# The chunk inverse of a bidirectional recurrence: 64x64 corners of the array, with the transpose carried along

## The chip, the cores and the metric

One core of a Trainium2 chip runs the whole program. The metric is the device time in microseconds (us) of one execution. TensorE is called PE here (its weight loads PEld), VectorE DVE, ScalarE ACT, GpSimd POOL and SyncE SP, as the profile names them.

## The reference, cut to what matters

The reference is an encoder trunk of two layers on 256 tokens of 1024 channels, in float32: a bidirectional RWKV-7 recurrence, a mixture of experts, a dilated attention, a second mixture of experts. Only the recurrence is touched. For each of 16 heads of 64 channels and for both directions it computes

```python
def step(state, inp):
    r_t, w_t, k_t, v_t, a_t, b_t = inp
    sa = jnp.einsum('bhvk,bhk->bhv', state, a_t)
    state = (state * w_t[:, :, None, :]
             + sa[:, :, :, None] * b_t[:, :, None, :]
             + v_t[:, :, :, None] * k_t[:, :, None, :])
    y_t = jnp.einsum('bhvk,bhk->bhv', state, r_t)
    return state, y_t
```

## The kernel before

The 256 tokens of a head and direction are cut into four chunks of 64. Inside a chunk the steps depend on each other through a strictly triangular 64x64 matrix A, so the kernel works out (1 - A)^-1 of each chunk, and the recurrence (`recur`, L963) then goes over only four chunks. Heads go in pairs, i = 0 to 7: two heads, two directions and four chunks are 16 inverses of 64x64 in one call of `inverse` (L882). They lie as 8 numbers n by two halves q of the 128 partitions, 64 columns each.

`chunks` (L828) leaves A in two half-precision parts. Before the change these tiles, Ah and Al (L690), are 128 wide: half q has its 64x64 block at columns 64q, so that tile [:, n, :] is a 128x128 matrix with two blocks on the diagonal, and zero elsewhere (cleared once by POOL, L692). Ah has had 1 subtracted (L853). `inverse` keeps T, the transposed inverse of ever larger blocks, 64 columns wide (`plain`, L895, an ACT copy from PSUM to half precision), and TTd, the same matrix not transposed and spread onto the diagonal (`spread`, L904, two ACT copies of one half each). Each of the levels l = 1 to 5 does: T from PSUM; for l > 1 a turn of T on PE (`turn`, L890: 16 matmuls of 64x64 weights against an identity) and its spread into TTd; Ah times T (`pairs`, L885: 8 matmuls with 128x128 weights and 64 columns); Q, that product under the level's mask, by DVE (L929); TTd times Q. At the end T is turned once more into X, the residual is taken with Ah and Al, split into TTd and Td, and two terms of its series are added (L954 to L960).

Work of several kinds is woven in the recurrence's phase (`weave`, L272, loop at L1158). Turn i has the streams steps(i) = recur(i) and then ready(i + 2) (scaled operands and chunk products), inverse(i + 1), finish(i - 1) (head norm, gate), and supply(i + 3) (the projections kr and v of a later pair, and shares of the modulations). Each emits its pieces with a priority that follows its share of PE's work (SHARE, L33), and a scheduler sets each engine's order at build time from those priorities. All engines run in that order. Names in the rows: iv is a PSUM bank of the inverse, cst (or cst16) the constants, kr and v the projections, wring the ring of weights, G the chunk products, R, U, S, Y the recurrence's banks, bb and sT the bonus, Al and Ah the parts of A, wo the output projection, gu and dn the experts' products. All matmuls are issued by one helper, at L266. A float32 matmul stands in the profile as two records.

The ring of weights (`Stream`, L120) gets more memory as tiles of this phase are given back (`later`, L1810, at i = 4, 5, 6, 7 and the end). The experts' weights, 1 MB a block, go into it.

Of the kernel before, what the change touches and what calls it, by code (L numbers as in the profile page):

```python
# [12 lines left out]
F16 = mybir.dt.float16  # L13
# [18 lines left out]
# share of the tensor engine's work of the streams that are woven, and their offset in priority  # L32
# [13 lines left out]
def _constants():  # L46
# [3 lines left out]
    parts = {}  # L50
# [4 lines left out]
    # from here on for the recurrence only  # L55
# [52 lines left out]
def _attn_constants():  # L108
    """Negative distances under the masks of the three groups; the tokens in the order even, odd."""
# [10 lines left out]
class Stream:  # L120
    """Blocks of weights, in the order in which they are used, through a ring of tiles.

    While a phase leaves room, a second pool lengthens the ring for the blocks before `limit`."""
# [38 lines left out]
    def spare(self):  # L162
        """A tile of the ring, once it holds all the blocks that are left."""
# [8 lines left out]
    def take(self, *names):  # L172
        """The next blocks; those taken before are used up."""
# [8 lines left out]
    def done(self):  # L182
        """The blocks taken last are used up."""
# [7 lines left out]
# modulations (layer, kind, eighth) that are worked out before and during each token mixer  # L191
# [45 lines left out]
def trunk(ctx, tc, names, aps, out, stages=("rwkv", "moe0", "attn", "moe1"), dbg=None, ring=2):  # L237
# [16 lines left out]
    def banks(**n):  # L254
        """The banks of PSUM of a phase, by their uses."""
# [16 lines left out]
    def weave(*streams):  # L272
        """Emits streams side by side, each in step with its share of the tensor engine's work."""
# [87 lines left out]
    def ada_first(tag, acc):  # L361
        """Shift and scale of the first norm, by both engines."""
# [23 lines left out]
    def ada(i, m, k, tag="ps"):  # L386
        """An eighth of one of the six modulations."""
# [31 lines left out]
    def split(hi, lo, src, by, eng=None):  # L419
        """src times `by` (a power of two) as the sum of two numbers in half precision"""  # L420
# [12 lines left out]
    def scales(i, which):  # L433
        """columns of the modulated norm: scale, shift"""
# [23 lines left out]
    def normalised(xn, tags):  # L458
        """the normalised stream in [d, t], two eighths of the channels in a bank each"""
# [17 lines left out]
    def transposed(j, behind=False):  # L477
        """a quarter of the stream's channels in [d, t]"""
# [9 lines left out]
    class Router:  # L488
        """Logits of the router, as the parts of x come in: its scale per token is put to the products."""
# [5 lines left out]
        def start(self):  # L495
            """The scaled weights, the part of the shift."""
# [14 lines left out]
        def hold(self, tag):  # L511
            """The bank and the sums that the parts of x go to."""
# [3 lines left out]
        def feed(self, t, c, junk):  # L516
            """a tile of tokens, half of the channels"""
# [23 lines left out]
    def gated(w, gate, k):  # L541
        """the rows of an output projection (k blocks side by side), times the gates of its columns"""
# [8 lines left out]
    def add_out(ps, t, c, by=1.0):  # L551
        """x += ps * by, in half of the channels of a tile of tokens"""
# [5 lines left out]
    def ada_share(n, tag="ps"):  # L558
        """The next n eighths of the modulations that go with layer 0."""
# [5 lines left out]
    def rwkv(pool):  # L565
# [4 lines left out]
        # (what the even pairs of heads use is given back before what the odd ones use)  # L570
# [5 lines left out]
        def pieces(tag):  # L576
            """tiles that are used before the recurrence needs their places"""
# [36 lines left out]
        # (past the ends lies a zero, which the shift does not move)  # L614
# [36 lines left out]
        def hidden():  # L651
            """LoRA hidden layers, [rank, t]"""
# [33 lines left out]
        E16, N16, R16 = cst16[:, 0:128], cst16[:, 128:256], cst16[:, 256:320]  # L686
        lv = cst16[:, 320:704].rearrange("p (l n) -> p l n", l=6)
        lv0 = cst16[:, 704:832]
        # (two matrices of 64 x 64 each, on the diagonal)
        Td, TTd, *A16 = [inv.tile([128, 8, 128], F16, name=n)  # L690
# [1261 lines left out]
```

## Time and profile before

| what | value |
|---|---|
| runs of the kernel | 1224.38, 1223.29 and 1211.89 us, median 1223.29 |
| span of the profiled execution | 1225.3 us (no time of that execution is given beside it) |
| PE, matmuls | 1086.9 us busy, 89%, 9460 records |
| PE, weight loads | 725.7 us, 59% |
| DVE | 660.5 us, 54% |
| ACT | 449.9 us, 37% |
| POOL | 177.8 us, 15% |
| mean granted PE clock | 0.936 |

Matmuls are pipelined and their ends modelled, so the distance between starts says what a matmul costs, not its own duration. The recurrence's phase is about the first 500 us; the experts of layer 0 follow to about 720 us, the attention to about 1000 us, the experts of layer 1 to the end.

### The profile page before, as it was taken

The page shows a single profiled execution, that of the slowest core. Times are in us where ns is not written, and L with a number is a line of the kernel's source. Part 1 is how long each engine was busy: PE and PEld are TensorE (multiplying, and loading weights), DVE is VectorE, ACT ScalarE, POOL GpSimd, SP SyncE. Part 2 cuts the span into 40 slices and gives each one's busy share as a digit, 9 for nine tenths or more (in the row PEclk, how much of TensorE's full clock was granted, in tenths as well). Part 3 has the DMA queues.
Part 4 walks back from the last instruction along what each step waited for, and adds up shares of the span by engine and source line. Part 5 has one row for each costly group of instructions (what it writes and reads, how often), then busy time and mean ns, then how long its engine had stood idle before and what let it go on. Part 6 is the DMA issues. An engine that isn't in the chain of part 4 may idle for free. (4 is left out here: it accounts for less than half of the span.)

```text
span 1225.3 us, 22879 instructions
## 1 busy us (share of the span) xinstructions
PE 1086.9 (89%) x9460; PEld 725.7 (59%) x9460; DVE 660.5 (54%) x1453; ACT 449.9 (37%) x940; POOL 177.8 (15%) x128
## 2 busy tenths in 40 slices
PE   4679999999999899897988879899988998799886
PEld 4556777777777664543443258778877864354432
DVE  8875477787774733522121166989986563122112
ACT  3326454464562552210010066546544531011002
POOL 6600001001120610000000012212283200000000
PEclk8789999999995999898998989989998999999989
DMA  9253164344352055898999996887653498989995
GB/s 373 101 206 117 35 204 125 123 156 133 106 173 103 2 241 221 333 422 352 422 421 421 420 419 240 315 319 290 237 197 138 168 361 358 417 366 421 421 420 229
DMA packets 53188, 322.46 MB, mean 263 GB/s; under 512 B 5922, under 2 KB 6562, under 8 KB 21458
## 3 DMA queue, kind: packets, MB, share of 16 engines
q1 hardware_dynamic: 51986, 316.49, 66.3%
q0 software_dynamic: 512, 2.30, 0.5%
q10 hardware_dynamic: 576, 2.10, 0.5%
q8 instruction: 78, 1.28, 0.4%
q14 instruction: 36, 0.29, 0.1%
HBM read 319.82 MB, written 1.05 MB: 262 GB/s over the span
## 5 line engine op out<-in xcount | busy, mean ns | idle before, releaser
L266 PE MATMUL gu<-wring,xT 128*32 128x512 f32 x1024 | 132.5, 619 | 16.9 <-DMA wring<-in_w_moe_dram 9.9
L358 DVE SCALAR_TENSOR_TENSOR acc<-aring,silu,acc 128x512 f32<-128x512 f32 x140 | 114.4, 849 | 9.5 <-DMA aring<-in_w_ada_dram 9.3
L425 POOL TENSOR_TENSOR wl<-wring,wh 128x1024 f16<-128x1024 f32 x24 | 57.2, 2383 | 407.1 <-DMA wring<-in_w_qkv_dram 241.0
L266 PE MATMUL qkv<-hl,wh 128*128 128x256 f16 x384 | 106.3, 277 | 2.0 <-DVE hl L1614 2.0
L266 PE MATMUL qkv<-hh,wl 128*128 128x256 f16 x384 | 106.4, 278 | 1.8 <-DVE wl L431 1.8
L266 PE MATMUL qkv<-hh,wh 128*128 128x256 f16 x384 | 106.6, 278 | 1.6 <-ACT hh L1613 1.6
L266 PEld LDWEIGHTS gu<-wring,xT 128*32 128x32 f32 x1024 | 31.8, 112 | 99.9 <-issue 80.4
L266 PEld LDWEIGHTS <-wh 128*128 128x128 f16 x768 | 76.4, 100 | 13.1 <-issue 3.6
L431 DVE SCALAR_TENSOR_TENSOR wl<-wring,wh 128x1024 f16<-128x1024 f32 x56 | 74.0, 1327 | 16.4 <-ACT wh L427 16.3
L266 PE MATMUL dn<-wring,hidT 128*32 128x256 f32 x1024 | 66.3, 407 | 18.1 <-ACT hidT L1416 18.0
L266 PE MATMUL acc<-y,back 128*128 128x512 f32 (+1 forms) x144 | 66.0, 581 | 10.3 <-DVE y L1443 8.1
L427 ACT ACTIVATE wh<-wring 128x1024 f16<-128x1024 f32 x56 | 58.6, 1050 | 35.4 <-PE qkv L266 30.8
L266 PEld LDWEIGHTS xT<-oh,x 128*128 128x128 f32 x512 | 59.0, 192 | 21.1 <-issue 9.2
L1218 DVE SCALAR_TENSOR_TENSOR sg<-sg,gu 128x256 f32<-128x256 f32 x16 | 6.7, 420 | 119.1 <-ACT sg L1217 119.1
L1443 DVE TENSOR_TENSOR y<-dn,ga 128x512 f32<-128x512 f32 x28 | 19.4, 692 | 88.9 <-PE dn L266 57.4
L266 PE MATMUL xT<-oh,x 128*128 128x128 f32 x512 | 63.5, 280 | 2.5 <-DVE oh L1327 2.5
L1217 ACT ACTIVATE sg<-gu 128x256 f32<-128x256 f32 x16 | 6.1, 383 | 153.1 <-PE gu L266 153.1
L266 PEld LDWEIGHTS dn<-wring,hidT 128*32 128x32 f32 x1024 | 32.1, 116 | 48.5 <-ACT hidT L1416 21.9
L1359 ACT ACTIVATE back<-bT 128x256 f32<-128x256 f32 x16 | 6.1, 384 | 131.7 <-PE acc L266 131.7
L266 PE MATMUL qkv<-wl,hh 128*128 128x256 f16 x192 | 54.0, 281 | 0.4 <-POOL wl L425 0.4
L266 PE MATMUL qkv<-wh,hl 128*128 128x256 f16 x192 | 53.9, 281 | 0.0
L266 PE MATMUL qkv<-wh,hh 128*128 128x256 f16 x192 | 53.9, 281 | 0.0
(341 smaller groups left out, 2292.0 us busy)
## 6 DMA issues: line engine op xcount, KB each, us to landing
wring<-in_w_moe_dram SPq DMA_DIRECT2D x192, 1024.0 KB, 19.8
aring<-in_w_ada_dram SPq DMA_DIRECT2D x96, 512.0 KB, 4.0
wring<-in_w_qkv_dram SPq DMA_DIRECT2D x36, 1024.0 KB, 8.5
wring<-in_w_kr_dram SPq DMA_DIRECT2D x8, 1024.0 KB, 5.1
wring<-in_w_vl_dram SPq DMA_DIRECT2D x8, 704.0 KB, 4.1
wring<-in_w_rwo_dram SPq DMA_DIRECT2D x4, 1024.0 KB, 5.9
wring<-in_w_ato_dram SPq DMA_DIRECT2D x4, 1024.0 KB, 6.5
ga<-in_p_adab_dram ACTq DMA_DIRECT2D x4, 512.0 KB, 3.8
```

What stands on the lines that cost most here:

```text
L266: return nc.tensor.matmul(out=o, lhsT=lhsT, rhs=rhs, start=start, stop=stop, **kw)
L358: V.scalar_tensor_tensor(out=acc[:, s], in0=w[:, s], scalar=silu[:, k:k + 1], in1=acc[:, s], op0=ALU.mult, op1=ALU.add)
L425: eng.tensor_tensor(out=lo, in0=src, in1=hi, op=ALU.subtract)
L427: A.activation(out=hi, in_=src, func=AF.Copy, scale=by)
L431: V.scalar_tensor_tensor(out=lo, in0=src, scalar=by, in1=hi, op0=ALU.mult, op1=ALU.subtract)
L1217: A.activation(out=o, in_=ps[:, 0:256], func=AF.Tanh, scale=0.5)
L1218: V.scalar_tensor_tensor(out=o, in0=o, scalar=1.0, in1=ps[:, 0:256], op0=ALU.add, op1=ALU.mult)
L1359: A.activation(out=back, in_=ps[:, 0:S], func=AF.Copy)
L1443: V.tensor_tensor(out=y, in0=py[c], in1=gates[i, 5][:, c * 512:(c + 1) * 512], op=ALU.mult)
```

## The change

The two blocks of a pair of halves are no longer spread onto the diagonal of a 128x128 matrix. Each 64x64 block is multiplied by itself, on the corner of the array that its half of the partitions belongs to (`blocks`: 16 matmuls for what 8 did). X, the inverse not transposed, is no longer got by turning T at each level: PSUM gets a second product, Q times X, beside X times Q, and ACT copies both (T and X, each 128 wide by 64 columns times 8). The clearing of the wide tiles goes. The residual's two parts are called E and T. Lines of the changed kernel are a few lower.

```diff
-    return np.concatenate([np.eye(128), -np.eye(128), e, np.concatenate([lv, lv], 0),
-                           np.kron(np.eye(2), lv[:, 0:64])], 1).astype(np.float16)
+    return np.concatenate([e, -e, np.concatenate([lv, lv], 0)], 1).astype(np.float16)
...
-        Td, TTd, *A16 = [inv.tile([128, 8, 128], F16, name=n)
-                         for n in ("Td", "TTd", "Ah0", "Al0", "Ah1", "Al1")]
-        for t in (*A16, Td, TTd):
-            P.memset(t, 0.0)
+        A16 = [inv.tile([128, 8, 64], F16, name=n) for n in ("Ah0", "Al0", "Ah1", "Al1")]
...
-                V.tensor_tensor(out=h, in0=h, in1=N16[half(q), 64 * q:64 * q + 64].unsqueeze(1).unsqueeze(1)
-                                .to_broadcast([64, 4, 2, 64]), op=ALU.add)
+            V.tensor_tensor(out=Ah, in0=Ah, in1=N16.unsqueeze(1).to_broadcast([128, 8, 64]), op=ALU.add)
...
-            def pairs(ps, lhsT, rhs, start, stop):
-                for n in range(8):
-                    mm(ps[:, n * 64:(n + 1) * 64], lhsT[:, n, :], R16 if rhs is None else rhs[:, n, :],
-                       start=start, stop=stop, skip_group_check=True)
-            def turn(ps, t):
+            def blocks(ps, lhsT, rhs, start=True, stop=True):
                 for n in range(8):
                     for q in range(2):
-                        mm(ps[half(q), n * 64:(n + 1) * 64], t[half(q), n, :], R16[half(q), :])
+                        mm(ps[half(q), n * 64:(n + 1) * 64], lhsT[half(q), n, :],
+                           R16[half(q), :] if rhs is None else rhs[half(q), n, :],
+                           start=start, stop=stop, skip_group_check=True)
+            def ones(ps, rhs):
+                for q in range(2):
+                    mm(ps[half(q)].rearrange(n8, m=64), R16[half(q), :], rhs[half(q)], start=True, stop=False,
+                       skip_group_check=True)
...
-            V.tensor_tensor(out=TTd, in0=Ah, in1=lv0.unsqueeze(1).to_broadcast([128, 8, 128]), op=ALU.mult)
+            X = tile16("X16")
+            V.tensor_tensor(out=X, in0=Ah, in1=lv[:, 0, :].unsqueeze(1).to_broadcast([128, 8, 64]), op=ALU.mult)
             pT = square()
-            pairs(pT, TTd, None, True, True)
+            blocks(pT, X, None)
             for l in range(1, 6):
                 yield
                 T = plain(pT, "T16")
                 if l > 1:
-                    px = square()
-                    turn(px, T)
-                    spread(TTd, px)
-                    yield
+                    X = plain(pX, "X16")
                 ps = square()
-                pairs(ps, Ah, T, True, True)
+                blocks(ps, Ah, T)
...
                 pT = square()
-                pairs(pT, TTd, Q, True, True)
+                blocks(pT, X, Q)
+                if l < 5:
+                    pX = square()
+                    blocks(pX, Q, X)
             yield
             T = plain(pT, "T16")
+            ps = square()
+            ones(ps, R16.unsqueeze(1).to_broadcast([128, 8, 64]))
+            blocks(ps, Ah, T, False, False)
+            blocks(ps, Al, T, False, True)
             px = square()
-            turn(px, T)
+            blocks(px, T, None)
+            yield
+            Eh, El = plain(ps, "E16"), tile16("T16")
+            V.tensor_tensor(out=El, in0=ps.rearrange(n8, m=64), in1=Eh, op=ALU.subtract)
             X = plain(px, "X16")
...
-            spread(TTd, ps)
-            for q in range(2):
-                V.tensor_tensor(out=parts(Td)[q], in0=ps[half(q)].rearrange(n8, m=64), in1=parts(TTd)[q],
-                                op=ALU.subtract)
             pd = square()
-            pairs(pd, TTd, X, True, True)
+            blocks(pd, Eh, X)
...
-            pairs(pF, TTd, X, False, False)
-            pairs(pF, Td, X, False, False)
+            ones(pF, X)
+            blocks(pF, Eh, X, False, False)
+            blocks(pF, El, X, False, False)
             yield
-            pairs(pF, TTd, Dd, False, True)
+            blocks(pF, Eh, Dd, False, True)
```

The scheduler sets a new order on every engine. The first place is PE's order at the end of the inverse of heads 2 and 3, before the change: the residual's products on the whole array (TTd and Td are the residual's parts there), with projections kr between them.

```order
L266 MATMUL iv<-X_1590,TTd 128x64
L266 MATMUL kr<-xr,wring 128x256
L266 LDWEIGHTS TTd
L266 MATMUL iv<-X_1590,TTd 128x64
L266 MATMUL kr<-xr,wring 128x256
L266 LDWEIGHTS Td
L266 MATMUL iv<-X_1590,Td 128x64
L266 LDWEIGHTS Td
L266 MATMUL iv<-X_1590,Td 128x64
```

The same place of the same inverse after the change (E and T are the residual's parts, Q its square's term).

```order
L265 MATMUL v<-xv,wring 128x256
L265 LDWEIGHTS T_1959
L265 MATMUL iv<-X_1961,T_1959 64x64
L265 MATMUL v<-xv,wring 128x256
L265 LDWEIGHTS E_1957
L265 MATMUL iv<-Q_1996,E_1957 64x64
L265 MATMUL v<-xv,wring 128x256
L265 MATMUL sT<-bb,cstr 128x256 x2
L265 MATMUL G<-AR,BK 128x128 x4
L265 LDWEIGHTS E_1957
L265 MATMUL iv<-Q_1996,E_1957 64x64
L265 MATMUL v<-xv,wring 128x256
```

In both, single matmuls of the inverse alternate with single projections; what stands in between is now a 64x64 corner, where it was a matmul on the whole array.

The second place is ACT's order in the first levels of that inverse, before the change: T, then the two half copies into TTd.

```order
L897 ACTIVATE T_1360<-iv 128x512
L988 ACTIVATE UV<-U 64x128 x2
L862 ACTIVATE BT<-BT,cstr 128x512
L907 ACTIVATE TTd<-iv 64x8x64
L908 ACTIVATE TTd<-iv 64x8x64
L748 ACTIVATE at<-at,a0h 128x256 x2
L897 ACTIVATE T_1414<-iv 128x512
```

After the change, T and X of a level stand next to each other.

```order
L899 ACTIVATE T_1567<-iv 128x512
L899 ACTIVATE X_1569<-iv 128x512
L899 ACTIVATE T_1680<-iv 128x512
L899 ACTIVATE X_1682<-iv 128x512
L755 ACTIVATE vT<-v 128x256
```

Three copies a level became two, and the copy of X no longer waits for a product of the copy of T.

## Rows read from the trace of the kernel before

**Rows 1.** The page, parts 1 and 2: busy time by engine; 40 slices.
```profile
PE 1086.9 (89%) x9460; PEld 725.7 (59%) x9460; DVE 660.5 (54%) x1453; ACT 449.9 (37%) x940; POOL 177.8 (15%) x128
PE   4679999999999899897988879899988998799886
```
**Rows 2.** Busy us by stretch: PE, PEld, DVE, ACT, POOL, PEclk, DMA share, GB/s.
```profile
130.00:178.00 48.00, 47.92 (x490) 36.04 (x489) 28.12 (x72) 27.28 (x57) 2.54 (x2) 1.00 0.38 126
178.00:226.00 48.00, 47.14 (x508) 35.58 (x507) 36.25 (x88) 25.20 (x54) 4.74 (x4) 0.96 0.45 138
226.00:274.00 48.00, 47.70 (x499) 35.42 (x500) 37.43 (x87) 26.03 (x56) 4.79 (x4) 0.96 0.42 136
274.00:322.00 48.00, 47.81 (x518) 34.98 (x517) 39.40 (x94) 28.16 (x60) 4.41 (x4) 1.00 0.47 147
322.00:370.00 48.00, 45.06 (x494) 33.56 (x492) 32.67 (x74) 23.43 (x52) 10.27 (x8) 0.96 0.37 126
370.00:401.00 31.00, 31.00 (x144) 23.80 (x146) 11.65 (x36) 8.24 (x18) 3.04 (x3) 0.51 0.26 102
401.00:430.00 29.00, 25.51 (x345) 18.58 (x346) 22.52 (x44) 16.66 (x35) 18.80 (x16) 1.00 0.01 2
430.00:462.00 32.00, 31.90 (x429) 20.14 (x427) 11.55 (x24) 17.35 (x37) 2.89 (x3) 1.00 0.57 231
...
500.00:740.00 240.00, 205.43 (x1630) 104.66 (x1630) 68.84 (x187) 44.58 (x102) 6.34 (x3) 0.95 0.97 401
```
**Rows 3.** The inverse's tile iv: duration min/median/max, first and last start, forms.
```profile
L266 PE MATMUL iv<-cst,T x640: 192/193/259, 100.0 to 455.4; 64*64 64x64 f16 x160
L266 PE MATMUL iv<-Q,TTd x384: 189/193/203, 98.8 to 461.3; 128*128 128x64 f16 x192
L266 PE MATMUL iv<-cst,TTd x64: 193/193/261, 96.4 to 433.0; 128*128 128x64 f16 x64
L907 ACT ACTIVATE TTd<-iv x40: 573/590/592, 100.5 to 456.5; 64x512 f16<-64x512 f32 x40
L947 DVE TENSOR_TENSOR Td<-iv,TTd x16: 674/689/695, 118.1 to 458.4; 64x512 f16<-64x512 f32 x16
```
**Rows 4.** Timeline of PE, 150 to 165 us: start, duration (us), instruction.
```profile
150.34 0.44 PE L266 MATMUL iv<-cst,T 64*64 64x64 f16 x16
150.71 0.41 PE L266 MATMUL iv<-T,Ah 128*128 128x64 f16 x8
...
159.31 3.62 PE L266 MATMUL kr<-xk,wring 128*128 128x256 f32 x16
...
165.15 0.68 PE L266 MATMUL kr<-xr,wring 128*128 128x256 f32 x2
```
**Rows 5.** Timeline of PE, 196 to 200 us.
```profile
196.11 0.70 PE L266 MATMUL kr<-xk,wring 128*128 128x256 f32 x2
196.65 0.40 PE L266 MATMUL iv<-T,Ah 128*128 128x64 f16 x8
196.88 0.63 PE L270 MATMUL BT<-cst,BK 128*128 128x128 f32 x4
...
198.79 0.40 PE L266 MATMUL iv<-Q,TTd 128*128 128x64 f16 x8
199.12 0.43 PE L266 MATMUL S<-SD,cst 64*64 64x128 f32 x2
```
**Rows 6.** Timeline of DVE, POOL and PE, 361 to 370 us (idle time before, releaser).
```profile
361.61 0.15 DVE L332 SCALAR_TENSOR_TENSOR rsq<-rsq 128x4 f32<-128x4 f32 x1
362.28 5.30 POOL L548 TENSOR_TENSOR wring<-wring,ga 128x512 f32<-128x512 f32 x4 [5.37 <-PE Y L266]
362.43 1.24 DVE L334 TENSOR_TENSOR rsq<-rsy 128x4 f32<-128x4 f32 x1
365.03 0.39 PE L266 MATMUL iv<-X,cst 128*128 128x512 f16 x1 [0.90 <-DVE Td L947]
369.92 0.79 PE L266 MATMUL sT<-bb,cstr 128*128 128x256 f32 x1 [2.05 <-DVE bb L815]
```

More of the change, by code (lines that the diff above doesn't have):

```diff
@@ L685, in rwkv @@
         sgn = cs("sgn")
-        E16, N16, R16 = cst16[:, 0:128], cst16[:, 128:256], cst16[:, 256:320]
-        lv = cst16[:, 320:704].rearrange("p (l n) -> p l n", l=6)
-        lv0 = cst16[:, 704:832]
-        Td, TTd, *A16 = [inv.tile([128, 8, 128], F16, name=n)
-                         for n in ("Td", "TTd", "Ah0", "Al0", "Ah1", "Al1")]
-        for t in (*A16, Td, TTd):
-            P.memset(t, 0.0)
+        R16, N16 = cst16[:, 0:64], cst16[:, 64:128]
+        lv = cst16[:, 128:512].rearrange("p (l n) -> p l n", l=6)
+        A16 = [inv.tile([128, 8, 64], F16, name=n) for n in ("Ah0", "Al0", "Ah1", "Al1")]
         eb = sup.tile([128, 528], F32, name="eb", bufs=1)
@@ L849, in chunks @@
                 a = gv[half(q), :, 1 - q::2, :]
-                h, l = (t.rearrange("p (g a) m -> p g a m", a=2)[half(q), :, :, 64 * q:64 * q + 64] for t in (Ah, Al))
+                h, l = (t.rearrange("p (g a) m -> p g a m", a=2)[half(q)] for t in (Ah, Al))
                 A.copy(out=h, in_=a)
                 P.tensor_tensor(out=l, in0=a, in1=h, op=ALU.subtract)
-                V.tensor_tensor(out=h, in0=h, in1=N16[half(q), 64 * q:64 * q + 64].unsqueeze(1).unsqueeze(1)
-                                .to_broadcast([64, 4, 2, 64]), op=ALU.add)
+            V.tensor_tensor(out=Ah, in0=Ah, in1=N16.unsqueeze(1).to_broadcast([128, 8, 64]), op=ALU.add)
             BT = turns(i, [128, 2, 2, 2, 128], "BT")
@@ L882, in inverse, with tile16 @@
         def inverse(i, w):
-            def pairs(ps, lhsT, rhs, start, stop):
-                for n in range(8):
-                    mm(ps[:, n * 64:(n + 1) * 64], lhsT[:, n, :], R16 if rhs is None else rhs[:, n, :],
-                       start=start, stop=stop, skip_group_check=True)
-            def turn(ps, t):
+            def blocks(ps, lhsT, rhs, start=True, stop=True):
                 for n in range(8):
                     for q in range(2):
-                        mm(ps[half(q), n * 64:(n + 1) * 64], t[half(q), n, :], R16[half(q), :])
+                        mm(ps[half(q), n * 64:(n + 1) * 64], lhsT[half(q), n, :],
[5 more added lines that the diff above has]
+                       skip_group_check=True)
+            def tile16(name):
+                return inv.tile([128, 8, 64], F16, name=name)
             def plain(ps, name):
-                t = inv.tile([128, 8, 64], F16, name=name)
+                t = tile16(name)
                 A.activation(out=t.rearrange("p n m -> p (n m)"), in_=ps, func=AF.Copy)
                 return t
-            def parts(t):
-                return [t[half(q), :, 64 * q:64 * q + 64] for q in range(2)]
-            def spread(t, ps):
-                a, b = parts(t)
-                A.activation(out=a, in_=ps[half(0)].rearrange(n8, m=64), func=AF.Copy)
-                A.activation(out=b, in_=ps[half(1)].rearrange(n8, m=64), func=AF.Copy)
             def square():
@@ L921, in inverse @@
                 if l > 1:
-                    px = square()
-                    turn(px, T)
-                    spread(TTd, px)
-                    yield
+                    X = plain(pX, "X16")
                 ps = square()
-                pairs(ps, Ah, T, True, True)
-                Q = inv.tile([128, 8, 64], F16, name="Q16")
+                blocks(ps, Ah, T)
+                Q = tile16("Q16")
                 V.tensor_tensor(out=Q, in0=ps.rearrange(n8, m=64),
@@ L932, in inverse @@
                 pT = square()
-                pairs(pT, TTd, Q, True, True)
+                blocks(pT, X, Q)
+                if l < 5:
+                    pX = square()
+                    blocks(pX, Q, X)
             yield
             T = plain(pT, "T16")
+            ps = square()
+            ones(ps, R16.unsqueeze(1).to_broadcast([128, 8, 64]))
+            blocks(ps, Ah, T, False, False)
+            blocks(ps, Al, T, False, True)
             px = square()
-            turn(px, T)
+            blocks(px, T, None)
+            yield
+            Eh, El = plain(ps, "E16"), tile16("T16")
+            V.tensor_tensor(out=El, in0=ps.rearrange(n8, m=64), in1=Eh, op=ALU.subtract)
             X = plain(px, "X16")
-            yield
-            ps = square()
-            mm(ps.rearrange(n8, m=64), E16, R16.unsqueeze(1).to_broadcast([128, 8, 64]), start=True, stop=False, skip_group_check=True)
-            pairs(ps, Ah, T, False, False)
-            pairs(ps, Al, T, False, True)
-            yield
-            spread(TTd, ps)
-            for q in range(2):
-                V.tensor_tensor(out=parts(Td)[q], in0=ps[half(q)].rearrange(n8, m=64), in1=parts(TTd)[q],
-                                op=ALU.subtract)
             pd = square()
-            pairs(pd, TTd, X, True, True)
+            blocks(pd, Eh, X)
             yield
@@ L953, in inverse @@
             pF = square()
-            mm(pF, E16, X.rearrange("p n m -> p (n m)"), start=True, stop=False, skip_group_check=True)
-            pairs(pF, TTd, X, False, False)
-            pairs(pF, Td, X, False, False)
+            ones(pF, X)
+            blocks(pF, Eh, X, False, False)
+            blocks(pF, El, X, False, False)
             yield
-            pairs(pF, TTd, Dd, False, True)
+            blocks(pF, Eh, Dd, False, True)
             TT = turns(i, [128, 8, 64], "TT")
```

## The prediction

> **What bounds the kernel now.** The first view to read is the busy share by engine over the span, with the forty slices [rows 1]: TensorE (PE) leads with 89%, and it is dense from the fourth slice on. The second is the same sum cut at the stretches of the recurrence [rows 2]. The change touches only layer 0's chunk inverses, so the reader should look at the six stretches from 130 to 370 us and from 430 to 462 us, in which they run: PE is busy 47.92, 47.14, 47.70, 47.81 and 45.06 of 48 us, and 31.90 of 32. VectorE (DVE) has 28 to 39 of 48, ScalarE (ACT) 23 to 28. Busy PE is no proof by itself, since ends of matmuls are modelled; but the timelines [rows 4, 5] show starts that follow each other with nothing between. So from 130 to 462 us, apart from some 10 us, the time is the length of PE's queue: what lengthens the queue lengthens the kernel, and what shortens an ACT or DVE chain does not shorten it. Behind 500 us the experts' weights bound the time (DMA share 0.97 to 740 us [rows 2]), but their transfers wait for memory that the recurrence gives back: the DMA share is 0.01 from 401 to 430 us. A later recurrence shifts them whole.
>
> **What the inverse costs on PE before and after.** The view by tile [rows 3] gives the matmuls of the eight inverses: 640 on 64\*64 corners, and on the whole array with 64 columns six rows of 384, 384, 128, 64, 64 and 64 (a first and a last are shown), 1088 together. Per inverse that is 80 and 136; two with 512 columns come to them by the code. By the code, after the change it is 22 groups of 16 corners = 352, and 4 corner matmuls of 512 columns.
> Prices, from starts [rows 4]: 16 corners last 0.44 us from the first start to the last end, 0.19 of it the last one's own, so 15 starts in 0.25 us, 0.0167 each. Eight whole-array matmuls that meet a matmul of the same array shape behind them: 196.65 to 196.88, 0.029 each [rows 5]. So two corners run side by side, and a group of 16 corners costs 0.27 us where 8 whole matmuls cost 0.23. Before: 136 x 0.029 + 80 x 0.0167 + 2 x 0.21 = 5.7 us an inverse; after: 352 x 0.0167 + 2 x 0.21 = 6.3 (the wide ones in pairs). First term: 0.6 x 8 = +5 us.
>
> Here a rule speaks against the change. The trace first: the corners of both halves write the same PSUM bank, and 16 of them start in 0.25 us [rows 4]. The Trainium skill, TensorEngine Tiling (Array Packing), Restrictions and Gotchas, says that different row tiles can't reach one PSUM bank at the same time; by that, corners would not overlap. The measured start distance disagrees with the rule for these two corners. A second one: the Trainium skill, TensorE: Matmul & The Clock Gate, Weight-path perf modes, gives the fast weight load only to 128 columns of weights; the trace has 0.0167 us for each corner's load and matmul all the same, so it does not add a term here. I keep what would follow if corners with two different operands did not overlap as a rival.
>
> **The cost that decides: changes of array shape.** A matmul on another shape (rows by columns of the array, as the profile prints them: 64\*64, 128\*64, 64\*128, 128\*128) does not follow closely. 198.79 to 199.12 is 0.33 us for eight matmuls before a 64\*64 one, against 0.23 before a 128\*128 one [rows 5]: 0.10 more. From the last corner's start (150.34 + 0.44 - 0.19 = 150.59) to the next whole-array start is 0.12 instead of 0.03 [rows 4]: 0.09 more. I take 0.095 us a change. Counted down the two built orders of PE, up to the first matmul of the experts, there are 522 such changes before and 728 after. Beside matmuls of the inverse 153 become 423; elsewhere 369 become 305. The places shown with the change say why: before, single inverse matmuls alternate with projections (kr, v) on the same whole array for nothing; now each alternation is two changes. Second term: 206 x 0.095 = +19.6 us.
>
> There is a third, smaller one. When PE returns to float32 from another group, the first matmul's second part (the profile has two records for one float32 matmul) starts 0.30 to 0.32 us after the first (0.68 and 0.70 us for two records, less 0.38 for the last one), not the 0.216 of a running series ((3.62 - 0.38)/15) [rows 4, 5]. The inverse stands in PE's order in 115 unbroken pieces before and in 275 after, so 160 more returns at about 0.08 = 13 us, less about 6 us for the 64 changes that go elsewhere (0.08 to 0.10 each). Third term: +7 us.
>
> **What goes.** ACT loses the two half copies onto the diagonal at each of five places (10 x 0.59 us) and gains four copies of X and one of the residual (5 x 0.59): 19 become 14 copies an inverse, 3 us less. DVE's three wide steps (0.69 each) become two narrower ones, some 1 us less. POOL loses six clearing steps at the start, which lie ahead of waits. All of this lies beside a full PE, so I cost it at nothing; it would pay only where PE waits. Those waits are few: 0.90 us for Td and 2.05 us for bb are the ones that can be read [rows 6]; they and others lie in the stretches 322 to 370 and 401 to 430, where PE is idle for 48 - 45.06 and 29 - 25.51, 6.4 us in all, and the other five have 1.5 us between them [rows 2]. A PE that comes some 3 us later per inverse finds these data ready. I take 7 of these 8 us. At nothing the sum is 7 higher.
>
> Sum: 5 + 19.6 + 7 - 7 = about +24 us. The profiled span is 1225.3 us and the median of the runs is 1223.29, 2.0 below it. 1225.3 + 24 - 2 = 1247 us.
>
> Bounds. The piece that no row shows is a whole inverse in corners in this denser mix. Low end: the third term at nothing and the waits in full, 5 + 19.6 - 7 = +18. High end: nothing from the waits, and returns at 0.10 on all 160: 5 + 19.6 + 16 = +41. So the likeliest case spans 1241 to 1264.
>
> **Rivals.**
> *The long clock dip goes.* From 370 to 401 us the granted clock is 0.51 [rows 2], the lower of its two levels (1.2 of 2.4 GHz), right after PE had waited 0.90 and 2.05 us [rows 6]. Those waits came from DVE, whose steps on 128x4 elements last 1.24 instead of 0.15 us while POOL multiplies the output weights for 5.30 us [rows 6]. If a later PE finds bb ready, the clock may stay up. Price: 31 x 0.49 = 15 us if all of the stretch followed the clock; I take 12 of it as an estimate. 1247 - 12 = 1235 us. For it: the wait is shorter than PE's new delay. Against: POOL's order keeps those multiplications at the same place.
> *The chain pays.* If the inverse's chain of copies, not PE, set each turn, 5 copies less an inverse would give 8 x 3 = 24 us, less the first term: 1223 + 5 - 24 = 1204 us, faster. It decides if PE's starts show idle before inverse matmuls; they show almost none [rows 5], and PE is 47 to 48 of 48 us busy [rows 2].
> *Corners don't overlap with two operands.* Then each takes 0.029 instead of 0.0167: 352 x 8 x 0.012 = 34 us more: 1281 us. Against: 640 corners overlap today [rows 4].
> *Hidden behind the weights.* If the experts' transfers set the end by themselves, nothing shows: 1224 us. Against: DMA share 0.01 and 0.57 in the stretches ahead of 462 us [rows 2].
> *The clock falls more often.* More short waits at shape changes could bring more stretches at the lower level; one more like that of 370 to 401 us costs 12: 1259 us.
>
> **How the numbers follow.** Likeliest case 0.64; long dip gone 0.15; chain pays 0.05; no overlap 0.04; hidden 0.06; clock falls more 0.06. One per cent (12 us) is about what a measurement of this kernel can tell from no change. Slower by over 1% (above 1235.5): 0.64 + half of 0.15 + 0.04 + 0.06 = 0.81; faster by over 1%: 0.05; the rest, 0.14, within 1%. The range of 8 in 10 reaches down into the dip's case and up past the likeliest's own high end: 1230 to 1268.
>
> **What would show it.** In the changed kernel's profile: the inverse's tile has 2848 matmuls, corners about 0.016 us apart inside a group; the step from a corner to a projection is about 0.095 us longer than before; the stretch from the first inverse's start to the last one's end, 365 us before, is 20 to 30 us longer; ACT's busy time is about 24 us less with no gain from it; what follows is shifted unchanged. Wrong would be: PE with gaps in which it waits for ACT's copies of T or X, corners 0.03 us apart, or a recurrence no longer than before.

## The result, and the profile after

| | before | after |
|---|---|---|
| runs, us | 1224.38, 1223.29, 1211.89, 1224.41, 1212.10 | 1266.58, 1284.68, 1284.93, 1279.29, 1278.91 |
| median, us | 1223.29 | 1279.29 |
| ratio | | 1.0531 (95% interval 1.0471 to 1.059): slower |
| profiled execution | span 1225.3 | time 1266.58, span 1264.8 |
| mean granted clock of the runs after, in their order | | 0.938, 0.916, 0.914, 0.925, 0.931 |

The forecast was 1247 us, with a range of 1230 to 1268. The sign was right; the median lies 56 us above before, not 24, and 11 us above the range. The profiled execution is the fastest of the five, and 39.5 us of span above that of before.

The first view is the page of the changed kernel, parts 1 and 2, as in [rows 1]: busy time by engine, 40 slices of PE's busy tenths, and 40 slices of the granted clock in tenths; below it the clock's row of the kernel before.
```profile
PE 1130.5 (89%) x10564; PEld 741.1 (59%) x10564; DVE 647.6 (51%) x1437; ACT 426.0 (34%) x900; POOL 165.8 (13%) x122
PE   5689999999998999987998879989897998799886
PEclk9979998999998779999899999998998999999989
```
```profile
PEclk8789999999995999898998989989998999999989
```
PE has 43.6 us more, which is more than the whole rise of the span (39.5); ACT 23.9 less, of which nothing shows in the time. The clock's row falls to 8, 7 and 7 in slices 13 to 15 (379 to 474 us), where before it falls to 5 in slice 13 alone.

The tile view of iv, as in [rows 3]: duration in ns (min/median/max), first and last start, and the shape (the count at the end of a line is that of a sample).
```profile
L265 PE MATMUL iv<-T,Ah x768: 186/193/257, 98.0 to 497.3; 64*64 64x64 f16 x192
L265 PE MATMUL iv<-Q,X x640: 186/193/259, 99.4 to 494.1; 64*64 64x64 f16 x160
L265 PE MATMUL iv<-X,Q x512: 192/193/238, 99.7 to 489.8; 64*64 64x64 f16 x171
L265 PE MATMUL iv<-cst,X x128: 192/193/213, 96.5 to 475.4; 64*64 64x64 f16 x128
L265 PE MATMUL iv<-Q,E x128: 186/213/260, 120.8 to 502.3; 64*64 64x64 f16 x128
L899 ACT ACTIVATE T<-iv x48: 575/597/597, 97.0 to 494.6; 128x512 f16<-128x512 f32 x48
```
All products are corners now (iv<-Q,X is the product that gives T, iv<-X,Q the one that carries its transpose). From the first inverse matmul to the last it is 502.3 - 96.5 = 405.8 us, before 461.3 - 96.4 = 364.9 [rows 3]: 40.9 us more. That is all of it, as the stretches show (busy us by stretch, columns as in [rows 2]; one inverse after another, the last row the experts):
```profile
145.00:205.00 60.00, 59.66 (x633) 42.22 (x632) 34.47 (x84) 25.57 (x53) 2.30 (x2) 0.91 0.42 139
205.00:259.00 54.00, 53.10 (x653) 37.23 (x654) 33.88 (x92) 23.08 (x51) 4.49 (x4) 0.94 0.35 112
259.00:310.00 51.00, 50.24 (x635) 34.09 (x629) 35.59 (x87) 23.16 (x51) 4.57 (x4) 1.00 0.40 130
...
395.00:399.00 4.00, 1.05 (x10) 0.61 (x5) 4.00 (x8) 0.30 (x1) 1.40 (x1) 1.00 0.00 0
399.00:426.00 27.00, 27.00 (x125) 19.84 (x125) 9.66 (x30) 7.38 (x15) 7.79 (x7) 0.50 0.40 157
426.00:457.00 31.00, 26.88 (x457) 17.93 (x455) 18.23 (x27) 12.06 (x29) 12.19 (x10) 0.94 0.01 2
457.00:474.00 17.00, 17.00 (x120) 13.15 (x119) 7.00 (x24) 5.36 (x11) 2.30 (x2) 0.51 0.04 7
...
540.00:780.00 240.00, 206.16 (x1627) 104.23 (x1627) 68.65 (x180) 44.70 (x101) 6.33 (x3) 0.95 0.98 404
```
The experts' 240 us are what they were (PE 206.16 against 205.43, DMA share 0.98 against 0.97), only 40 us later. In the recurrence PE is still full. The long stretch at the lower clock level has stayed (399 to 426 us at 0.50, after PE was busy only 1.05 of 4 us; before it was 370 to 401 us), and a second one of 17 us, from 457 us, is new. Shorter falls at 191 and 249 us (10.2 and 6.8 us, before 3.4 each at 192 and 240) are behind the 0.91 and 0.94 of the first two rows.

The whole of the recurrence in one row each, before (96 to 461 us), then after (96 to 502 us):
```profile
96.00:461.00 365.00, 356.07 (x3756) 261.20 (x3757) 236.56 (x556) 191.41 (x405) 51.48 (x42) 0.94 0.37 125
```
```profile
96.00:502.00 406.00, 392.49 (x4852) 273.35 (x4853) 227.29 (x542) 169.04 (x370) 50.59 (x42) 0.92 0.34 118
```
PE idles 406 - 392.49 = 13.5 us, before 365 - 356.07 = 8.9. The levels being 1 and 0.5, the mean clock says how long the lower one held: 2 x 0.08 x 406 = 65 us against 2 x 0.06 x 365 = 44 (the trace's own clock records, which the table below uses, give 68.3 and 44.4).

What a broken group looks like, from PE's timeline of the changed kernel:
```profile
153.20 1.56 PE L265 MATMUL v<-xv,wring 128*128 128x256 f32 x6
154.69 0.44 PE L265 MATMUL iv<-T,Ah 64*64 64x64 f16 x16
155.06 1.13 PE L265 MATMUL v<-xv,wring 128*128 128x256 f32 x4
...
178.63 0.70 PE L265 MATMUL v<-xv,wring 128*128 128x256 f32 x2
179.26 0.21 PE L265 MATMUL iv<-X,E 64*64 64x64 f16 x1
179.40 0.70 PE L265 MATMUL v<-xv,wring 128*128 128x256 f32 x2
...
183.85 0.21 PE L265 MATMUL iv<-Q,E 64*64 64x64 f16 x1
183.99 0.70 PE L265 MATMUL v<-xv,wring 128*128 128x256 f32 x2
```
Sixteen corners in one piece are over 0.37 us after their start (154.69 to 155.06), the step to the next array shape included. A single corner between two projections makes the step from v to v 0.77 us (178.63 to 179.40), where two records of a running series take 2 x 0.216 = 0.43: 0.34 us for one matmul of 64 columns. By the same measure the sixteen together cost 0.56 (from v to v 153.20 to 155.06, less six records of 0.216). The inverse stands in 275 pieces, 34 an inverse, and in the second half of each these are often single corners: in the order of starts 91 pieces are single corners in this trace, one in that with whole groups below, and 2 pieces are single matmuls in that of before. So the place shown with the change, where single matmuls of the old inverse alternate with projections, is a rare one in the kernel before.

### The profile page after: what moved, and what is told of

Read it like the earlier page. It is cut to its first block, busy times and chain, and to the rows that moved or that the text cites. A ratio compares the mean times of both kernels' runs of the same rounds, so it can differ in the third digit from the quotient of the medians.

```text
span 1264.8 us, 25047 instructions
## 1 busy us (share of the span) xinstructions
PE 1130.5 (89%) x10564; PEld 741.1 (59%) x10564; DVE 647.6 (51%) x1437; ACT 426.0 (34%) x900; POOL 165.8 (13%) x122
## 3 DMA queue, kind: packets, MB, share of 16 engines
HBM read 319.74 MB, written 1.05 MB: 254 GB/s over the span
## 5 line engine op out<-in xcount | busy, mean ns | idle before, releaser
L265 PE MATMUL gu<-wring,xT 128*32 128x512 f32 x1024 | 132.7, 621 | 16.0 <-PEq L1453 10.2
L265 PE MATMUL G<-AR,BK 64*128 64x128 f32 x256 | 52.3, 341 | 0.3 <-DVE AR L801 0.3
## 6 DMA issues: line engine op xcount, KB each, us to landing
wring<-in_w_moe_dram SPq DMA_DIRECT2D x192, 1024.0 KB, 19.8
```

The source lines that it names most:

```text
L265: return nc.tensor.matmul(out=o, lhsT=lhsT, rhs=rhs, start=start, stop=stop, **kw)
```

## The experiments

Theory A was that the cost lies in where the corners stand: each group cut by whole-array matmuls costs changes of array shape ("changes" below) and returns to float32, and the clock falls more. A "piece" is an unbroken row of inverse matmuls in PE's order. B: the second product, which carries the transpose, makes the loss. C: the shorter chain pays. D: the 1104 additional matmuls cost by themselves. E, F and G are told with their runs. The kernel before was run beside each set: 1224.37 us in the first, 1221.83 in the second, 1222.40 in the third.

**Corners without the carried transpose.** The kernel before, its products as corners of the same wide tiles:
```
-  mm(ps[:, n * 64:(n + 1) * 64], lhsT[:, n, :], R16 if rhs is None else rhs[:, n, :], ...)
+  for q in range(2):
+      mm(ps[half(q), n * 64:(n + 1) * 64], lhsT[half(q), n, 64 * q:64 * q + 64],
+         R16[half(q), :] if rhs is None else rhs[half(q), n, :], ...)
```


> The kernel before, with the eight whole-array matmuls of each product replaced by sixteen corner matmuls on the two diagonal blocks of the same wide tiles; turning, spreading and all of ScalarE's and VectorE's work stay. Counted in PE's built order up to the experts: 700 changes of array shape (522 before, 728 in the changed kernel) and 224 unbroken pieces of inverse matmuls (115 and 275). Theory A (corners between whole-array matmuls cost array-shape changes, and the thinner PE work lets the clock fall more often; carrying the transpose along is not the cause): 178 x 0.095 = 17 for the changes, 5 for the corners, 5 for float32 returns, and 10 to 25 for the clock, so 1250 to 1275 us against 1223 before. Rival B (the second product that carries the transpose, with its extra bank and its place in ScalarE's order, makes the loss): 1222 to 1235 us.

Measured: 1271.69 us, ratio 1.042 (1.0363 to 1.0476). Nearly the whole loss comes with the corners alone; ScalarE's copies, the turning and the wide tiles are as before. B falls.

**The changed kernel, its transpose turned.**
```
+  pX = square(); blocks(pX, T, None); X = plain(pX, "X16"); yield      # at each level from the second
...
-  pX = square(); blocks(pX, Q, X)                                      # the carried product
```


> The changed kernel, but the transpose X is got at each level by turning T with sixteen corner matmuls, as the kernel before did, in place of the carried product; 695 changes of array shape and 240 pieces (728 and 275 with the carried one), the same 2848 inverse matmuls. Theory A: near the changed kernel, 1262 to 1285 us, since the corners stay. Rival B (the carried product makes the loss): falls back to 1225 to 1240 us. Rival C (the shorter chain is worth something, and the loss lies elsewhere): 15 us or more above the changed kernel, 1295 or more.

Measured: median 1282.97 us of four runs, 1257.35, 1281.86, 1284.08 and 1289.07. All lie above what B gave (1225 to 1240) and below what C gave (1295 or more), so neither shows; whether the longer chain costs something smaller can't be told in this spread.

**The same change, its groups left whole.** One number of the weave's table:
```
-OFFSET = dict(W=1, C=-0.2, R=-0.5, S=0, F=0.3, A=0)
+OFFSET = dict(W=1, C=-0.2, R=-1.5, S=0, F=0.3, A=0)
```


> The changed kernel with one number of the weave altered: the inverse's priority offset goes from -0.5 to -1.5, so its groups stand unbroken in PE's order. 569 changes of array shape and 104 pieces, against 728 and 275 in the changed kernel and 522 and 115 before; the same matmuls and the same chain. Theory A: 47 x 0.095 = +4.5 for the changes, +5 for the corners, nothing for returns, and the clock much as before: 1222 to 1245 us. Rival D (the 1104 additional matmuls, or corners as such, are the cost, wherever they stand): 1262 to 1285 us.

Measured: 1224.51 us, ratio 1.0014 (0.9984 to 1.0044). The loss is gone, with every corner still there. D falls. Its PE timeline at the end of an inverse, where the changed kernel has the single corners shown above:
```profile
163.91 0.42 PE L265 MATMUL iv<-X,T 64*64 64x64 f16 x16
164.29 0.35 PE L265 MATMUL iv<-Q,E 64*64 64x64 f16 x11
164.45 0.27 PE L265 MATMUL R<-vc,GV 64*64 64x64 f32 x2
164.48 0.26 PE L265 MATMUL iv<-Q,E 64*64 64x64 f16 x5
```
What cuts a group here is R, of the same array shape. And the row of its recurrence (96 to 462 us):
```profile
96.00:462.00 366.00, 355.35 (x4861) 257.43 (x4857) 223.76 (x541) 167.36 (x370) 51.20 (x42) 0.95 0.37 125
```
The stretch is 366 us with 4861 matmuls, as long as before with 3756; ACT has 24 us less than before, and it is worth nothing.

**The control: the same number in the kernel before.**

> The kernel before with the same priority number, -1.5 for -0.5: 523 changes of array shape and 112 pieces, as good as the 522 and 115 before. All theories: the time before, 1212 to 1232 us. Should it come out faster or slower by more than 1%, the number itself is worth that, and the run of the changed kernel with it is to be read against this one.

Measured: 1222.21 us, ratio 1.0031 (0.9995 to 1.0068). The number by itself does nothing here, but it also changes little here: the old inverse stood in 115 pieces and now stands in 112, with 476 changes for 475. So this run does not show what cuts of whole-array groups cost. Nor does the pair of runs show that the cuts alone are the cause, since in the changed kernel the number moves the whole weave; that they go with the loss rests on the order by pieces below. Beside this, the new inverse at its best is no faster than the old one.

**In between and beyond: offsets -0.7 and 0.**

> The changed kernel with the priority offset -0.7: 670 changes of array shape and 187 pieces, between those of -1.5 (569, 104) and of the changed kernel (728, 275). Theory A (changes of shape, returns to float32 and the clock that falls with them): 5 for the corners + 148 x 0.095 = 14 + some 3 for returns = 22, and 5 to 20 for the clock, so 1246 to 1266 us where the kernel before has 1224. Theory A2 (only a few particular places count, the ones at which the clock falls, and the number of changes is beside the point): no order with the count, as near 1224 or 1279 as between.

> The changed kernel with the priority offset 0: 773 changes of array shape and 388 pieces, the most of all. Theory A: 5 + 251 x 0.095 = 24 + some 8 for returns = 37, and 15 to 35 for the clock: 1275 to 1297 us, at or above the changed kernel's 1279. Theory A2: no order with the count; below 1270 would speak for it.

Measured: 1241.55 us (ratio 1.0146, 1.0081 to 1.0211) and 1284.09 us (1.0507, 1.045 to 1.0563). With the changed kernel that makes an order by pieces: 104, 187, 275, 388 give 1224.5, 1241.6, 1279.3, 1284.1 (the last two overlap: single runs go from 1266.6 to 1284.9 and from 1278.1 to 1293.4). The run of -0.7 came out 4 us under what A gave. A2, by which the count is beside the point, falls.

**What the clock and the waits are worth: the gate moved to the output.**
```
-  w = gated(stream.take(("rwo", 0, c)), gates[0, 2][:, c * 512:(c + 1) * 512], 4)   # GpSimd
+  w = stream.take(("rwo", 0, c))
...
+  def add_gated(ps, t, c):                                                          # VectorE
+      V.tensor_tensor(out=ps, in0=ps, in1=gates[0, 2][:, c * 512:c * 512 + 512], op=ALU.mult)
+      add_out(ps, t, c)
...
```
The second half of the weights goes the same way. The expectations speak of 24 products on GpSimd; the trace of before has 16 (wring<-wring,ga, 362 to 417 us).

> The changed kernel, with the output weights no longer multiplied by the gate on GpSimd (24 products of 128x512); the gate is applied to the eight output blocks on VectorE instead, before they are added (8 more steps of 0.7 us, four of them at the end). The inverse's place in PE's order stays: 721 changes, 275 pieces. It asks what the clock is worth: VectorE is no longer slowed beside GpSimd, so PE does not wait 3 us twice (before 399 and 440 us), and the stretch of 27 us at half clock from 399 us should go, that of 17 us from 457 us perhaps. Theory A with a price of about 0.45 us for each us at half clock: 12 for the long stretch + 5 for the waits - 3 for the steps at the end = 10 to 22 us below the changed kernel run beside it, 1257 to 1269. Rival E (the half clock there costs nothing that shows, PE's array-shape changes are all): within 5 us of 1279.

Measured: 1260.33 us, ratio 1.0292 (1.0218 to 1.0366), in the range of A. The wait is gone: the tile view of sT in the recurrence (its matmuls; PE's idle time before them, us and times) has in the changed kernel
```profile
L265 PE MATMUL sT<-bb,cstr x28: 379/379/634, 130.6 to 440.1; 128*128 128x256 f32 x28
its engine sat idle before it (us, times) until:
  DVE bb L810: 5.5, 2
```
and with the gate on the output no such line. The long stretch at the lower level from 399 us is gone too. But that run's profile shows other stretches in its place, 75.1 us at the lower level in all where the changed kernel's profile has 68.3, so the edit does not show by itself what the clock is worth. The two profiles side by side do: in both, PE's matmuls are the same by name and shape for the first 4116, up to 426 us. Here are 96 to 110 and 110 to 135 us of the changed kernel, then of this one:
```profile
96.00:110.00 14.00, 12.59 (x252) 8.86 (x252) 4.24 (x8) 5.85 (x11) 0.00 (x0) 1.00 0.29 96
110.00:135.00 25.00, 24.86 (x260) 16.47 (x260) 12.08 (x34) 9.99 (x24) 0.00 (x0) 0.93 0.19 67
```
```profile
96.00:110.00 14.00, 12.98 (x257) 9.26 (x253) 3.59 (x6) 5.93 (x11) 0.00 (x0) 1.00 0.25 86
110.00:135.00 25.00, 25.00 (x192) 14.50 (x192) 8.71 (x26) 8.87 (x19) 0.00 (x0) 0.52 0.18 67
```
At 0.93 PE starts 260 matmuls in these 25 us, at 0.52 it starts 192 of the same order. From the start of one inverse to that of the next, in us, with the us at the lower level and PE's idle time behind it:

| inverse | after | after, gate |
|---|---|---|
| 1st | 48.9, 3.4, 1.1 | 57.7, 23.9, 1.1 |
| 2nd | 59.5, 10.2, 0.3 | 62.2, 16.3, 0.3 |
| 3rd | 53.8, 6.8, 0.9 | 58.2, 17.8, 0.9 |
| 4th | 51.2, 0.0, 0.8 | 51.2, 0.0, 0.8 |
| 5th | 50.9, 0.0, 1.1 | 50.9, 0.0, 1.1 |
| 6th | 66.1, 27.3, 4.1 | 52.0, 3.4, 0.8 |

Where neither has the lower level the times are equal; in the first three the idle time is equal too, and each us more at the lower level costs 0.40 to 0.45 us. In the sixth, 14.1 us less 3.3 of idle time for 23.9 us is 0.45 again. The order of PE is the same, so this is the clock's price. E falls.

**Both edits, and the gate alone.**

> Offset -1.5 and the gate on the output together: 563 changes, 104 pieces. Theory A: 1224 less the long stretch at half clock (24 us x 0.45 = 11) and the wait before it (3), plus 3 at the end: 1208 to 1218 us, faster than both kernels. Rival E: 1220 to 1228 us.

> The kernel before with the gate on the output blocks in place of GpSimd's 24 products; 526 changes of array shape (522 before), order otherwise kept. It asks what of the gain of the run with both edits is the gate's alone. Theory A: the 31 us at half clock from 370 us go or shrink, PE no longer waits 2 us for bb: 7 to 14 us under the kernel before, 1208 to 1217. Rival F (the gate pays only beside the new inverse): 1219 to 1226.

Measured: 1214.91 us, ratio 0.9942 (0.9908 to 0.9975), and 1208.87 us, ratio 0.9935 (0.9888 to 0.9982). Both lie some 0.6% below the kernel before, and are not told apart by their ratios, so the gain is the gate's, which the old inverse has as well (F falls); the new inverse adds nothing to it. Rows of their recurrences, the new inverse (96 to 451 us) and the old one (96 to 460 us in four stretches):
```profile
96.00:451.00 355.00, 346.61 (x4840) 250.86 (x4842) 219.40 (x543) 167.17 (x370) 29.22 (x26) 0.98 0.38 129
```
```profile
96.00:200.00 104.00, 102.10 (x1072) 76.72 (x1072) 62.30 (x154) 54.94 (x116) 4.84 (x4) 1.00 0.36 119
200.00:300.00 100.00, 98.84 (x1070) 72.70 (x1068) 79.71 (x185) 54.97 (x117) 10.89 (x9) 0.98 0.43 136
300.00:400.00 100.00, 99.38 (x1064) 75.00 (x1061) 67.52 (x171) 56.68 (x126) 9.97 (x9) 0.95 0.36 124
400.00:460.00 60.00, 58.35 (x680) 36.40 (x679) 29.90 (x74) 30.23 (x65) 6.28 (x6) 1.00 0.53 212
```
GpSimd's products are gone (29 us of POOL where it was 51), and the clock is up (0.98 for 0.95 in the new inverse; in the old one the lower level holds 13.7 us for 44.4).

**Fewer changes still: a miss.** The recurrence's offset C from -0.2 to -1 makes its pieces stand together too.

> Offset -1.5 and the gate on the output as in the run that has both, and the recurrence's offset from -0.2 to -1: 469 changes of array shape against 563, the same 104 pieces and the same matmuls. From the ten profiles so far the stretch from the first to the last inverse matmul is 285 us + 0.54 x (us at half clock) + 0.12 x (changes), within 4 us each; by that, theory A expects 94 x 0.12 = 11 us under the 1214.9 of that run: 1199 to 1210 us. Rival G (only changes beside the inverse's corners cost; those among the float32 pieces of the recurrence are hidden): 1211 to 1219.

> The kernel before with all three edits (inverse's offset -1.5, recurrence's -1, gate on the output): 435 changes against 526, 112 pieces. Theory A: 91 x 0.12 = 11 us under the kernel before with the gate alone: 1198 to 1208 us; and beside the changed kernel with the same three edits (469 changes, and the corners' own 5 us) 4 to 10 us faster. Rival C (the shorter chain of the new inverse pays once its corners stand together): slower than the changed kernel with the same edits.

> The changed kernel with the two offsets (-1.5 and -1) and the gate on GpSimd as it was: 469 changes, 104 pieces. Theory A: 100 x 0.12 = 12 under the 1224.5 of offset -1.5 alone: 1207 to 1218 us. Rival G: 1220 to 1228.

Measured: 1224.59 us (ratio 1.0086, 1.0042 to 1.0129), 1210.52 (0.9964, 0.9918 to 1.001) and 1229.52 (1.0113, 1.0007 to 1.022). All three are above what A gave, by 14, 2 and 11 us at least; the first is slower by 10 than with the recurrence at its old place, and G was wrong as well. The row of its recurrence (94 to 453 us), and the one from its last inverse matmul to the start of the experts' first sums (acc), 453.6 to 500.9 us; below them the latter stretch with C at -0.2, 451.6 to 492.2 us:
```profile
94.00:453.00 359.00, 339.05 (x4824) 249.75 (x4826) 219.34 (x537) 168.99 (x369) 30.41 (x26) 0.93 0.37 125
```
```profile
453.60:500.90 47.30, 46.23 (x266) 24.10 (x260) 25.29 (x80) 10.89 (x31) 1.99 (x2) 1.00 0.72 289
```
```profile
451.60:492.20 40.60, 39.84 (x250) 22.08 (x244) 22.34 (x75) 10.45 (x30) 1.99 (x2) 0.98 0.75 311
```
PE idles 20 us now, 8.4 with C at -0.2, the clock is at 0.93, where it was 0.98, and behind the last inverse come 47.3 us of work where there were 40.6. So the 12 us of changes that A counted as saved came back as lower clock, as waits, and as work behind the last inverse. That the recurrence's pieces, now ahead, had been filling waits is the likely reason, not a shown one. In the old inverse the same edit does nothing measurable.

**All profiles together.** Per kernel: the median; from its profile the stretch from the first to the last inverse matmul, us at the lower clock level in it, PE's idle time in it; from its built order the changes of array shape in that stretch (counted by starts in the trace they come out 1 to 10 more), and pieces of inverse matmuls.

| kernel | median us | stretch | lower level | idle | changes | pieces |
|---|---|---|---|---|---|---|
| before | 1223.3 | 364.9 | 44.4 | 8.5 | 475 | 115 |
| after | 1279.3 | 405.8 | 68.3 | 13.0 | 670 | 275 |
| corners alone | 1271.7 | 405.9 | 85.3 | 5.8 | 655 | 224 |
| after, turned | 1283.0 | 422.2 | 105.8 | 11.1 | 649 | 240 |
| after, R -1.5 | 1224.5 | 366.2 | 34.1 | 10.7 | 512 | 104 |
| before, R -1.5 | 1222.2 | 362.3 | 37.5 | 9.2 | 476 | 112 |
| after, R -0.7 | 1241.6 | 388.6 | 54.6 | 8.6 | 613 | 187 |
| after, R 0 | 1284.1 | 426.1 | 102.4 | 15.7 | 711 | 388 |
| after, gate | 1260.3 | 402.4 | 75.1 | 7.4 | 670 | 275 |
| after, R -1.5, gate | 1214.9 | 355.0 | 17.1 | 7.8 | 512 | 104 |
| before, gate | 1208.9 | 347.8 | 13.7 | 4.0 | 480 | 115 |
| after, R -1.5, C -1, gate | 1224.6 | 359.5 | 47.8 | 19.8 | 412 | 104 |
| before, R -1.5, C -1, gate | 1210.5 | 344.7 | 20.5 | 13.3 | 385 | 112 |
| after, R -1.5, C -1 | 1229.5 | 366.3 | 61.4 | 21.8 | 412 | 104 |

A least-squares fit through the fourteen gives the stretch as 284.8 + 0.54 x (lower level) + 0.12 x (changes); the largest miss is 3.7 us. It is a fit: the two numbers rise together in most of these kernels, so 0.54 may hold some of what is not clock; the same order at two clocks gave 0.40 to 0.45.

## Why the prediction was wrong, by its steps

**Right: what bounds the kernel, and where.** PE's queue between the first and the last inverse sets the time. All of the 39.5 us of span arise there (40.9, of which 1.4 come back behind it), and what follows is shifted. ACT's relief bought nothing, as forecast: 191 us became 169 in that stretch. The rivals "the chain pays", "corners don't overlap" and "hidden behind the weights" are out: the turned transpose changes nothing that can be told, sixteen corners are over after 0.37 us with two operands as with one, and the experts are unchanged.

**About right: the three terms of the queue.** They were 5 for the corners, 19.6 for 206 changes and 7 for float32 returns, 31.6 together. Measured in the profile it is 40.9 less 4.6 of idle time less the clock's 10 to 13 (24 us more at the lower level, at 0.43 to 0.54): 23 to 26. The forecast for these terms was 6 to 9 us too high. By the fit it is 195 changes x 0.12 = 23, returns within it. The third term, for returns, was not measured by itself. One reason given for the second does not hold: before, single inverse matmuls hardly alternate with projections (2 such pieces in the trace); the new inverse is cut far more often (91 single corners). The step from a corner to another shape, 0.12 us in place of 0.03 (154.94 to 155.06), is what [rows 4] had shown. The Trainium skill, TensorEngine Tiling (Array Packing), Key Properties, says that a change of tiling mode drains the engine; the trace agrees in that the step to another shape is longer, by 0.09 us here. The corners' own 5 us don't show as such: with whole groups the changed kernel stands 2.3 us above its control, and 46 changes more would explain 5 by themselves, so that term was probably too large.

**Wrong: "A PE that comes some 3 us later per inverse finds these data ready. I take 7 of these 8 us."** Idle time did not fall by 7, it rose by 4.6. The largest wait, for bb, grew from 4.5 us (the kernel before, the first two lines) to 5.5. [rows 6] had said why: POOL's multiplication of the output weights begins when a PE result (Y) releases it. A later PE makes POOL later too, and it meets the same VectorE steps: in the changed kernel the first of these products starts at 390.4 us, again behind a PE result (rn), 28 us later than before, and PE waits 2.95 us for bb where it waited 2.05.
```profile
L266 PE MATMUL sT<-bb,cstr x28: 379/379/792, 123.8 to 413.9; 128*128 128x256 f32 x28
  DVE bb L815: 4.5, 2
...
391.64 4.75 POOL L547 TENSOR_TENSOR wring<-wring,ga 128x512 f32<-128x512 f32 x3
391.96 1.23 DVE L334 TENSOR_TENSOR rsq<-rsq,rsh 128x4 f32<-128x4 f32 x1
398.66 1.57 PE L265 MATMUL sT<-bb,cstr 128*128 128x256 f32 x4 [2.95 <-DVE bb L810]
```
The gate's run of the changed kernel, in which these products are gone and the wait with them, shows that they are its cause.

**Wrong, and the larger miss: the clock at nothing.** The sum had no term for it. "The clock falls more often" was a rival with a chance of 0.06 and 12 us, and "the long dip goes" had 0.15. The dip stayed, since its wait stayed. In the profiled execution the lower level holds 24 us longer, 10 to 13 us of time. And the profiled one is the best of five: the median execution had a mean clock of 0.925 in place of 0.938, 2 x (0.075 x 1277.5 - 0.062 x 1264.8) = 35 us more at the lower level, and it is 12.7 us slower with the same program, 0.36 us for each. So of the 56 us 23 to 26 are the queue's, 5 waits and 23 to 26 the clock; of the clock's, the 12.7 between the profile and the median rest on the clocks of the runs alone, since only one execution was profiled. What was overlooked is that the clock also falls without a wait. The 0.96 in three stretches of [rows 2] are such falls: in the trace of before three of 3.4 us, at 192, 240 and 336 us, come with no idle time of PE in the 7 us ahead, among matmuls of many shapes (9, 14 and 15 changes in these 7 us; the 7 us are a length chosen for this reading). The changed queue has more of such places. In the profile of corners alone, eight of nine falls come with at most 0.2 us idle and 14 or more changes in the 7 us ahead, where that stretch has 11 on average, and its 85.3 us at the lower level go with less idle time (5.8 us) than the 44.4 of before (8.5).

That the clock falls because groups are broken is what the order by pieces speaks for: 104 to 115 pieces go with 14 to 44 us at the lower level where the recurrence's place was left alone, 187 with 55, 224 to 388 with 68 to 106. The price of the clock is shown by the two profiles of one order; that the broken groups bring the falls is an association over these kernels, and no edit was tried that moves the one without the other. It isn't the only thing that does: with C at -1, where the changes are fewest (385 to 412), nearly all the falls come behind waits, and the lower level holds 20 to 61 us. Nor is it settled what sets how long a fall lasts: one order gave 3.4 us in one profile and 24 in another.

## What to carry to other kernels

Before cutting whole-array matmuls into corners, look at what stands between them in PE's built order: corners beside each other cost about as much as the whole (with whole groups the two kernels are 2 us apart), but each cut by another array shape costs about 0.1 us twice and a float32 return besides; so give the cut stream a priority at which its groups stay whole, or leave the matmuls whole-array. Where PE's queue is the bound, price a change of its mix with the clock as well: the spread of time against granted clock over the runs one has gives a first size of that term. And a wait that another engine causes, when that engine is itself released by the late one, moves with it, so it isn't to be booked as gone.

## What the runs showed of the hardware that was not expected

- The same PE order ran 110 to 135 us once at 0.93 and once at 0.52, and over six inverses each us more at the lower level cost 0.40 to 0.45 us; with whole programs, five runs of the changed kernel spread over 18 us with mean clocks from 0.938 down to 0.914.
- One corner between two float32 projections costs 0.34 us; sixteen together at such a place cost 0.56.
- GpSimd's 16 products of 128x512 cost the kernel before 8 us by the ratio and 13 by the medians, though GpSimd is idle most of the time: beside them VectorE's steps of 128x4 take 1.2 us in place of 0.15 [rows 6], PE waits for bb, and the clock falls. The Trainium skill, SBUF — State Buffer, SBUF: two separate sides, says that a VectorE step with two inputs in SBUF and a GpSimd step that reads SBUF lock a shared pair of ports for a whole instruction. The traces agree: in none of the fourteen is one of these 128x4 steps of the recurrence longer than 0.3 us without a GpSimd step running beside it, and the slowed ones of [rows 6] last 1.1 to 1.2 us, where one product lasts 1.27.
- Fewer changes of array shape are no gain by themselves: 100 fewer, got by bringing the recurrence's pieces forward, made 10 us more.
